# A decoder step in split fp32: where the upper MLP inverts its token factors, and in what order the lower MLP's first group loads and multiplies

## The chip, the cores and the metric

The kernel runs on one NeuronCore of a Trainium2 chip. The engines are TensorE (PE, with its weight loads apart as PEld), VectorE (DVE), ScalarE (ACT), GpSimd (POOL) and SyncE (SP), which issues most of the DMA transfers. The metric is the device time of one execution in microseconds; lower is better.

## The reference

One inference step of a decoder trunk with one layer, for 1024 prompt tokens and 8 sample tokens that share the weights: a hybrid of differential attention and retention, cross-attention into a memory, then the MLP that the change is about, and a last RMSNorm.

```python
def rmsnorm(x, g):
    y = xf * lax.rsqrt(jnp.mean(xf * xf, axis=-1, keepdims=True) + EPS)
    return (y * g.astype(jnp.float32)).astype(x.dtype)

def sq_relu_mlp(h, w_up, w_down):
    return jnp.square(jax.nn.relu(h @ w_up)) @ w_down
...
        xp = xp + sq_relu_mlp(rmsnorm(xp, norm_mlp[l]), w_up[l], w_down[l])
...
    y_prompt = rmsnorm(xp, norm_final)
```

D_MODEL is 1024, the hidden width 4096. All values are fp32.

## The kernel before, in words

**Number format.** Each fp32 operand is split in two parts, high and low (a cast on ScalarE, a subtraction on VectorE), and a product takes three matmuls: high by high, high by low, low by high. Names: `UH`/`UL` and `T_h`/`T_l` are right operands (activations, columns are tokens), `wu` and `wd` are split left operands (128 x 1024, high half and low half) of the upper and the lower MLP.

**Seven products.** Both MLP products use a variant of Strassen's scheme: the matrices are cut in 2 x 2 blocks, and seven products (numbers 1 to 7) take the place of eight. The tokens are 1032 columns, cut in two halves and each in two chunks c = 0, 1 of QC = 258.

**Upper MLP.** `up_block(b, W, chunks)` does block b of 16. For each product q in the order 1, 6, 2, 7, 5, 4, 3 and each chunk it runs 12 matmuls into a PSUM bank of kind `X` (products 1, 2), `Z` (6, 7, 4) or `Y` (5, 3), two banks of each. VectorE forms `u2` after product 6 and `u3` after 7, each of which must be read out before the next product may accumulate into that bank. `hidden(quad, src, c)` takes the relu, multiplies it by the token factor in `ssum` (one over the RMS of the token, since the norm is applied behind the product), and ScalarE squares it into `hq`. After product 3, `hidden` stores three quarters of `hq` to HBM (`HQ`, from ScalarE's queue), GpSimd forms four differences `ht` and stores them (`HT`). `norm_factor(x)` computes the token factors of a quarter of the columns: a matmul with ones, a square root on ScalarE, a reciprocal on VectorE. It is called for quarters 0 and 1 before block 0, and for 2 and 3 between chunk 0 and chunk 1 of block 0; blocks 1 to 15 run both chunks.

**Lower MLP.** Four groups g of the hidden width. In each, stages of products (1, 2), (6), (7, 4), (5, 3); within a stage pairs of tiles p (0, 1, then 2, 3), and chunks c. A step (q, p, c) is a chain of 12 matmuls, `lower`, called `dn` in the trace; products 1 and 2 of one (p, c) use one bank one after the other. In group 0 ScalarE copies product 1 to the accumulator `c0`, then product 2 goes on in the same bank; all other results VectorE adds to the accumulators `c0`, `c11`, `c21`, `c22`, `c12`, of which the last four are first loaded with the residual (`residual_rows`). Operands:

- `raw_d{g}_{p}_{x}`: the raw left operands, two loads of 512 KB for each p (x = 0, 1). `left_lower(g, p, q)` splits them to `wd` (ring of eight tiles); for product 6 it forms differences in place, on VectorE and GpSimd.
- `raw_h{g}_{q}_{kk}`: the raw right operand of product q in two loads (kk = 0, 2) from `HQ` or `HT`, through a ring of three raw tiles of which `raw_d0_1_1` holds one in group 0. `right_lower(g, q)` issues them on SP and splits them into one of four slots of `UH`/`UL`.

**What sets the order.** A scheduler places the instructions on the five queues by the dependencies between tiles, with the order of TensorE's matmuls in the MLP pinned to that of the program (`pinned`). `tc.issue_after(x)` keeps what follows behind instruction x in that order. Tiles with one tag share memory, so a tile's first write waits for the last use of the tile that had the place before. The tiles `xq2_0`, `xq3_0` hold `hq` and `xq2_1`, `xq3_1` hold `ht` of chunks 0 and 1 through the upper MLP. PSUM has eight banks; `acc` tiles of the lower MLP take them in turns, the first tile where the allocator puts it. By the addresses as built, the first eight are banks 0, 7, 6, 5, 4, 1, 2, 3, and the upper MLP has `X` in 2 and 3, `Z` in 4 and 5, `Y` in 6 and 7.

In group 0, of the left operands' loads those of p = 0 are issued on SP and those of p = 1, 2, 3 on GpSimd's queue, p = 2 and 3 in tiles `xq2_0`, `rd2`, `xq3_0`, `rd3`.

Of the kernel before, what the change touches and what calls it, by code (L numbers as in the profile page):

```python
# [2 lines left out]

# [45 lines left out]
def decoder_step(ctx: ExitStack, tc: tile.TileContext, i: dict, o: dict):  # L49
    nc = tc.nc  # L50

    def pool(name, bufs=1, space=None, side=None):
        if space is None:
            return tc.tile_pool(name=name, bufs=bufs, reuse_waits="tile", side=side)
        if space is PSUM:
            return tc.tile_pool(name=name, bufs=bufs, space=space, reuse_waits="tile")
        return tc.tile_pool(name=name, bufs=bufs, space=space)
# [1580 lines left out]
    def norm_factor(x):  # L1638
        cs = QCOLS[x]
        fp = PD.tile([P, 512], F32, tag=("mk", "dt")[x % 2], name=f"rm_{x}", bufs=1)[:, :QC]  # L1640
        mm(fp, onesq, ssum[:, cs], True, True)
        rf = ssum[:, cs]
        nc.scalar.activation(rf, fp, AF.Sqrt, scale=1.0 / D, bias=epsc)
        nc.vector.reciprocal(rf, rf)

    def first_half(c):

# [135 lines left out]

    def up_block(b, W, chunks):

        HQ_ = {}
        Z, X, Y, p1, u2, u3 = {}, {}, {}, {}, {}, {}

        def bank(kind, c):
            return SP.tile([P, 512], F32, tag=kind, name=f"{kind}_{b}_{c}", bufs=2)[:, :QC]  # L1790

        def small(kind, c, bufs=2):
            return HP.tile([P, QC], F32, tag=kind, name=f"{kind}_{b}_{c}", bufs=bufs)

        def hidden(quad, src, c):
            if c not in HQ_:
                if (b, c) == (0, 0):
                    HQ_[c] = N.tile([P, 4, QC], F32, tag="hq0", name="hq_0_0")
                else:
                    HQ_[c] = N.tile([P, 4, QC], F32, tag=f"xq{2 + c}_0", name=f"hq_{b}_{c}")  # L1800
            h = HQ_[c]
            r = small("r", f"{quad}_{c}", 4) if quad == 11 else src
            nc.vector.scalar_tensor_tensor(r, src, 0.0, ssum[:, QCOLS[2 * c + HALF_OF[quad]]], ALU.max, ALU.mult)  # L1803
            nc.scalar.activation(h[:, PLACE[quad], :], r, AF.Square)  # L1804
            if quad == 12:
                nc.scalar.dma_start(HQ[b, c].rearrange("p (x j) -> p x j", x=3), h[:, 0:3, :])
# [4 lines left out]
                nc.gpsimd.tensor_sub(t[:, 1, :], h22, t[:, 0, :])  # L1811
                nc.gpsimd.tensor_sub(t[:, 2, :], h22, h12)
                nc.gpsimd.tensor_sub(t[:, 3, :], h21, t[:, 1, :])
                nc.gpsimd.dma_start(HT[b, c].rearrange("p (x j) -> p x j", x=4), t)

        for q in (1, 6, 2, 7, 5, 4, 3):
            for c in chunks:
                if q in (1, 6, 5):
                    kind, d = {1: ("X", X), 6: ("Z", Z), 5: ("Y", Y)}[q]
                    d[c] = bank(kind, c)  # L1820
                ps = (X if q in (1, 2) else Z if q in (6, 7, 4) else Y)[c]
                product(W, q, c, ps, q in (1, 6, 5))
                if q == 1:
                    p1[c] = small("p1", c)
                    nc.scalar.copy(p1[c], ps)  # L1825
                elif q == 6:
                    u2[c] = small("u2", c)
                    nc.vector.tensor_add(u2[c], ps, p1[c])  # L1828
                elif q == 2:
                    hidden(11, ps, c)  # L1830
                elif q == 7:
                    u3[c] = small("u3", c)
                    nc.vector.tensor_add(u3[c], ps, p1[c])
                else:
                    quad, x = {5: (22, u3), 4: (21, p1), 3: (12, u2)}[q]
                    r = small("r", f"{quad}_{c}", 4)
                    nc.vector.tensor_add(r, ps, x[c])
                    hidden(quad, r, c)
# [29 lines left out]
    STAGES = [(1, 2), (6,), (7, 4), (5, 3)]  # L1868
    SOURCE = {1: (HQ, 0), 2: (HQ, 1), 3: (HQ, 2), 5: (HT, 0), 6: (HT, 1), 7: (HT, 2), 4: (HT, 3)}
    taken = [0, 0]  # L1870
    with pool("acc", side="right") as AC, pool("w") as A, pool("w_ps", space=PSUM) as PS:
# [6 lines left out]
        def residual_rows(quad):  # L1878
            kh, hs = {11: (0, lo_h), 21: (4, lo_h), 22: (4, hi_h), 12: (0, hi_h)}[quad]
            nc.sync.dma_start(C[quad], X3[kh : kh + 4, :, hs].rearrange("k p c -> p k c"))  # L1880


        FINISH_AT, tails = {2: (0, 0), 5: (1, 0), 9: (0, 1), 15: (1, 1)}, {}
# [61 lines left out]
        def finish(c, half):  # L1945
            tail = tails[c] if half else None
            cs = QCOLS[2 * c + half]
            fp = PS.tile([P, 512], F32, tag="acc", name=f"fin_{c}_{half}", bufs=8)[:, :QC]
            mm(fp, onesq, ssf[:, cs], True, tail is None)
            if tail is not None:  # L1950
                mm(fp, onesq, tail, False, True)
            rf = A.tile([P, QC], F32, tag="rf", name=f"rf_{c}_{half}", bufs=2)
            nc.scalar.activation(rf, fp, AF.Sqrt, scale=1.0 / D, bias=epsc)
            for ft in range(8):
                y = C[((11, 21), (12, 22))[half][ft // 4]][:, ft % 4, c * QC : c * QC + QC]
                nc.scalar.activation(y, y, AF.Copy, scale=g_fin[:, ft : ft + 1])
            nc.vector.reciprocal(rf, rf)
            for kh in range(2):
                y = C[((11, 21), (12, 22))[half][kh]][:, :, c * QC : c * QC + QC]
                nc.vector.tensor_mul(y, y, rf.unsqueeze(1).to_broadcast([P, 4, QC]))  # L1960
                nc.sync.dma_start(o["yT"][4 * kh * P : (4 * kh + 4) * P, cs].rearrange("(f p) c -> p f c", p=P), y)

        pin[0] = True
        for g in range(4):
            raws = {}
            for p in range(4):
                u = U_DN + 8 * g + 2 * p
                raws[p] = [
                    N.tile([P, 1024], F32, tag=("t2", "hq0", "xq2_0", "xq3_0")[p], name=f"raw_d{g}_{p}_0"),

                    G.tile([P, T], F32, tag="raw", name="raw_d0_1_1", bufs=3) if (g, p) == (0, 1)
                    else N.tile([P, 1024], F32, tag=("t3", "xq2_1")[p], name=f"raw_d{g}_{p}_1") if p < 2
                    else A.tile([P, 1024], F32, tag=f"rd{p}", name=f"raw_d{g}_{p}_1"),
                ]
            for p, x in ((0, 0), (0, 1), (1, 0), (1, 1), (2, 0), (2, 1), (3, 0), (3, 1)):

                (nc.gpsimd if g == 0 and p else nc.sync).dma_start(raws[p][x][:, :1024], i["wall"][U_DN + 8 * g + 2 * p + x])
            for stage in STAGES:
                if (g, stage[0]) == (0, 1):
                    residual_rows(11)  # L1980
                S = {q: right_lower(g, q) for q in stage}
                if (g, stage[0]) == (0, 7):

                    with tc.issue_after(seen["SP"]):
                        for quad in (22, 21, 12):
                            residual_rows(quad)
                end = g == 3 and stage == (5, 3)
                batches = [(0, 1), (2, 3)] if len(stage) == 2 else [(0, 1, 2, 3)]
                if end:
                    batches = [(0, 1, 2, 3)]  # L1990
                bank = {}
                steps = [(q, p, c) for batch in batches for q in stage for p in batch for c in range(2)]
                if end:
                    steps = [(q, p, c) for c in range(2) for q in stage for p in range(4)]
                W = {}
                for n, (q, p, c) in enumerate(steps):
                    if (q, p) not in W:
                        W[q, p] = left_lower(g, p, q)
                    if q == stage[0]:
                        bank[p, c] = PS.tile([P, 512], F32, tag="acc", name=f"dn_{g}_{q}_{p}_{c}", bufs=8)[:, :QC]  # L2000
                    ps = bank[p, c]
                    lower(W[q, p], S[q], c, ps, q == stage[0])
                    cq = slice(c * QC, c * QC + QC)
                    y = C[INTO[q]][:, p, cq]
                    if g == 0 and q == 1:
                        nc.scalar.copy(y, ps)
# [208 lines left out]
```

## Time and profile before

| | us |
|---|---|
| three runs | 1546.4, 1548.47, 1551.26 (median 1548.47) |
| profiled execution | 1553.3 |
| its span | 1551.5 |
| granted TensorE clock, mean | 0.988 |
| last product of the upper MLP ends, first of the lower starts | 1203.83 |

The table's first row is the measure. The profile is of another execution, 4.8 us longer than the median, and its clock readings (start, duration) count from the start of its span. In the rows, a line number such as L1928 is that of the kernel before, `out<-in` are the tiles by name without numbers, `x3` is the number of instructions in the row, and the last bracket tells how long the engine was idle before and which instruction's end released it.

### The profile page before, as it was taken

Reading aid. Unit: us, or ns where it says so; the run is one execution under the profiler, and the core shown is the slowest. Engines: PE = TensorE matmul, PEld = TensorE weight load, DVE = VectorE, ACT = ScalarE, POOL = GpSimd, SP = SyncE. Lnnn points to the kernel's source line nnn. Section 1 sums busy time; section 2 is a strip of 40 time slices with the busy share of each in tenths; the row PEclk is TensorE's granted clock in tenths of the full one; section 3 lists DMA queues with packets and bytes.
Section 4 is the critical chain, followed back from the end, with each engine's and each line's share of the span. In section 5 each row is a group of like instructions: output and inputs, shape, how many; then the busy total and the mean of one; then the engine's idle time right before and its main releaser. Section 6 shows DMA issues by size and latency. Waiting matters only on the chain.

```text
span 1551.5 us, 26774 instructions
## 1 busy us (share of the span) xinstructions
PE 1494.2 (96%) x10483; PEld 1394.0 (90%) x10483; DVE 1072.6 (69%) x2096; ACT 651.0 (42%) x1267; POOL 440.8 (28%) x461
## 2 busy tenths in 40 slices
PE   9899999999999899999999899999999899999997
PEld 7678869999759899988899899999999799999996
DVE  4324513988865735566696988888788688787887
ACT  6323323665642332046634643333334444334454
POOL 0343302122533421124222234443335402020360
PEclk9999999999999999999999999999999999999999
DMA  8645334212766156451583334434335873636313
GB/s 291 171 116 156 78 104 115 82 51 69 235 215 240 48 202 180 138 183 64 182 269 129 101 138 151 151 138 150 137 138 172 293 232 86 197 82 198 96 42 110
DMA packets 121874, 230.02 MB, mean 148 GB/s; under 512 B 14209, under 2 KB 74480, under 8 KB 121620
## 3 DMA queue, kind: packets, MB, share of 16 engines
q1 hardware_dynamic: 91508, 170.30, 35.3%
q0 software_dynamic: 21024, 41.10, 8.6%
q10 hardware_dynamic: 9216, 16.91, 2.9%
q8 instruction: 82, 1.34, 0.4%
q14 instruction: 44, 0.36, 0.1%
HBM read 168.93 MB, written 57.52 MB: 146 GB/s over the span
## 4 chain that ended last, share of the span: by engine, by line
PE 63%; DVE 17%; DMA 11%; ACT 4%; issue 3%; POOL 1%; SPq 0%; DVEq 0%; ACTq 0%; POOLq 0%
PE dn L1928 17%; PE Z L1778 5%; PE mq L67 5%; PE pr_o L67 4%; PE qkp L67 4%; PE Y L1778 4%; PE vrp L67 3%; PE vap L67 3%; DVE wu L1617 3%; PE grp L67 3%; DMA raw_up<-in_wall 3%; PE X L1778 2%; PE pr_m L67 2%; PE sp L67 2%; PE av L67 2%
## 5 line engine op out<-in xcount | busy, mean ns | idle before, releaser
L1928 PE MATMUL dn<-UH,wd 128*128 128x258 f32 x1792 | 326.1, 284 | 7.7 <-ACT wd L1906 4.3
L1928 PEld LDWEIGHTS dn<-UH,wd 128*128 128x128 f32 x1792 | 278.2, 190 | 9.2 <-ACT wd L1906 4.7
L1928 PE MATMUL dn<-UL,wd 128*128 128x258 f32 x896 | 253.3, 283 | 0.0
L1928 PEld LDWEIGHTS dn<-UL,wd 128*128 128x128 f32 x896 | 169.7, 189 | 0.1
L1804 ACT ACTIVATE hq<-r 128x258 f32<-128x258 f32 x128 | 53.5, 419 | 162.8 <-DVE r L1803 162.8
L2008 DVE TENSOR_TENSOR c<-c,dn 128x258 f32<-128x258 f32 x216 | 88.4, 418 | 35.5 <-PE dn L1928 33.4
L1778 PE MATMUL Z<-T_h,wu 128*128 128x258 f32 x512 | 100.0, 287 | 7.0 <-DVE u L1828 5.3
L1906 ACT CAST wd<-raw_d 128x512 fp32r<-128x512 f32 x96 | 58.9, 618 | 102.6 <-PE dn L1928 84.5
L1617 DVE TENSOR_TENSOR wu<-raw_up,wu 128x512 fp32r<-128x512 f32 x96 | 92.0, 959 | 9.2 <-ACT wu L1616 9.2
L1778 PE MATMUL X<-UH,wu 128*128 128x258 f32 x512 | 97.7, 282 | 0.4 <-ACT p L1825 0.4
L110 DVE TENSOR_TENSOR wl_u<-raw_u,wh_u 128x1024 fp32r<-128x1024 f32 x46 | 59.8, 1308 | 50.9 <-ACT wh_u L109 49.0
L1778 PEld LDWEIGHTS Z<-T_h,wu 128*128 128x128 f32 x512 | 81.4, 189 | 10.4 <-DVE u L1828 8.3
L1907 DVE TENSOR_TENSOR wd<-raw_d,wd 128x512 fp32r<-128x512 f32 x96 | 75.5, 790 | 14.3 <-ACT wd L1906 14.2
L1778 PEld LDWEIGHTS X<-UH,wu 128*128 128x128 f32 x512 | 81.3, 188 | 0.7 <-ACT p L1825 0.7
L1900 DVE TENSOR_TENSOR UL<-raw_h,UH 128x1032 fp32r<-128x1032 f32 x56 | 77.3, 1381 | 6.4 <-ACT UH L1899 6.4
L109 ACT CAST wh_u<-raw_u 128x1024 fp32r<-128x1024 f32 x50 | 52.3, 1050 | 69.9 <-PE mq L67 43.2
L1899 ACT CAST UH<-raw_h 128x1032 fp32r<-128x1032 f32 x56 | 58.8, 1055 | 52.0 <-PE dn L1928 30.9
L1810 POOL TENSOR_TENSOR ht<-hq 128x258 f32<-128x258 f32 x32 | 22.3, 698 | 202.1 <-ACT hq L1804 188.1
L1920 POOL TENSOR_TENSOR raw_d<-raw_d,raw_d 128x512 f32<-128x512 f32 x16 | 23.3, 1456 | 179.5 <-DVE raw_d L1916 164.0
L1778 PE MATMUL Z<-T_l,wu 128*128 128x258 f32 x256 | 72.3, 282 | 0.0
L1778 PE MATMUL X<-UL,wu 128*128 128x258 f32 x256 | 72.3, 282 | 0.0
L1616 ACT CAST wu<-raw_up 128x512 fp32r<-128x512 f32 x96 | 57.1, 610 | 30.4 <-DVE raw_up L1623 23.7
(482 smaller groups left out, 4634.6 us busy)
## 6 DMA issues: line engine op xcount, KB each, us to landing
raw_u<-in_wall SPq DMA_DIRECT2D x59, 512.0 KB
HT<-ht POOLq DMA_DIRECT2D x32, 516.0 KB
raw_h<-HT SPq DMA_DIRECT2D x32, 516.0 KB
raw_up<-in_wall SPq DMA_DIRECT2D x32, 512.0 KB
raw_d<-in_wall SPq DMA_DIRECT2D x26, 512.0 KB
HQ<-hq ACTq DMA_DIRECT2D x32, 387.0 KB
raw_h<-HQ SPq DMA_DIRECT2D x24, 516.0 KB
cmk<-in_cmk SPq DMA_DIRECT2D x16, 512.0 KB
```

Source lines behind the costliest of these rows:

```text
L67: pinned(nc.tensor.matmul(out, l, r, start=start, stop=stop))
L110: (lo_engine or nc.vector).tensor_sub(wl[:, :n], raw[:, :n], wh[:, :n].bitcast(F32))
L1616: nc.scalar.copy(w[:, :512], src)
L1617: nc.vector.tensor_sub(w[:, 512:], src, w[:, :512].bitcast(F32))
L1778: pinned(nc.tensor.matmul(ps, l, r[:, k, :], start=first and k == 0 and x == 0, stop=k == 3 and x == 2, skip_group_check=True))
L1804: nc.scalar.activation(h[:, PLACE[quad], :], r, AF.Square)
L1899: nc.scalar.copy(h, rv)
L1900: nc.vector.tensor_sub(l, rv, h.bitcast(F32))
L1906: nc.scalar.copy(w[:, :512], src)
L1907: nc.vector.tensor_sub(w[:, 512:], src, w[:, :512].bitcast(F32))
L1928: pinned(nc.tensor.matmul(ps, l, r[:, k, cq], start=first and k == 0 and x == 0, stop=k == 3 and x == 2, skip_group_check=True))
L2008: nc.vector.tensor_add(y, y, ps)
```

## The change

1. *Upper MLP.* The reciprocal leaves `norm_factor` for a new function `invert(x)`. For quarters 2c and 2c + 1 it is called in block 0, ahead of `hidden` of product 2 and behind `u3` of product 7.
2. *Upper MLP, last block.* The four differences `ht` of (b, c) = (15, 1) are formed on VectorE.
3. *PSUM.* The lower MLP's banks get eight tags, `acc0` to `acc7`, placed in order and used in turns. As built, the first eight are banks 0 to 7.
4. *Left operands of group 0.* All raw loads are issued on SP: p = 0, 1 first, p = 2, 3 behind the loads for product 6 and `c11` (now loaded in two halves). p = 2 gets tiles `rd2`, `rd3` of a pool of its own, p = 3 gets `xq2_0` and `xq3_0`. 
5. *Order of group 0.* (1, 2) on p = 0, 1; (6) on p = 0, 1; then for p = 2 and for p = 3 (1, 2) and (6). What follows is as before. `issue_after` puts the splits of p = 2, 3 and the operands of products 7 and 4 behind ScalarE's copies, and the loads of `c22`, `c21` and `c12` one by one behind the right operands.

```diff
         rf = ssum[:, cs]
         nc.scalar.activation(rf, fp, AF.Sqrt, scale=1.0 / D, bias=epsc)
-        nc.vector.reciprocal(rf, rf)
+
+    def invert(x):
+        nc.vector.reciprocal(ssum[:, QCOLS[x]], ssum[:, QCOLS[x]])
...
-                nc.gpsimd.tensor_sub(t[:, 0, :], h12, h11)
...
+                eng = nc.vector if (b, c) == (15, 1) else nc.gpsimd
+                eng.tensor_sub(t[:, 0, :], h12, h11)
...
                 elif q == 2:
+                    if b == 0:
+
+                        invert(2 * c)
                     hidden(11, ps, c)
                 elif q == 7:
                     u3[c] = small("u3", c)
                     nc.vector.tensor_add(u3[c], ps, p1[c])
+                    if b == 0:
+                        invert(2 * c + 1)
...
+        turns = [0]
+        for x in BANK_ORDER:
+            PS.tile([P, 512], F32, tag=f"acc{x}", name=f"acc{x}_order", bufs=1)
+
+        def acc_bank(name):
+            turns[0] += 1
+            return PS.tile([P, 512], F32, tag=f"acc{(turns[0] - 1) % 8}", name=name, bufs=1)[:, :QC]
...
+                tags = (("t2", "t3"), ("hq0", "xq2_1"), ("rd2", "rd3"), ("xq2_0", "xq3_0"))[p]
...
-                (nc.gpsimd if g == 0 and p else nc.sync).dma_start(raws[p][x][:, :1024], i["wall"][U_DN + 8 * g + 2 * p + x])
...
+            load_left((0, 1) if g == 0 else range(4))
+            S, W, bank, copied = {}, {}, {}, {}
+
+            parts = [((1, 2), (1, 2), (0, 1)), ((), (1, 2), (2, 3)), ((6,), (6,), (0, 1)), ((), (6,), (2, 3))]
+            if g == 0:
+
+                parts = [((1, 2), (1, 2), (0, 1)), ((6,), (6,), (0, 1))] + [((), qs, (p,)) for p in (2, 3) for qs in ((1, 2), (6,))]
+            parts += [((7, 4), (7, 4), (0, 1)), ((), (7, 4), (2, 3)), ((5, 3), (5, 3), (0, 1)), ((), (5, 3), (2, 3))]
...
+                if g == 0 and 7 in new:
+
+                    for q, quad in ((7, 22), (4, 21)):
+                        with tc.issue_after(seen["SP"]), tc.issue_after(copied[2]):
+                            S[q] = right_lower(g, q)
+                        with tc.issue_after(seen["SP"]):
+                            residual_rows(quad)
...
+                if g == 0 and 1 in new:
+                    residual_rows(11, (slice(0, 2),))
+                if g == 0 and 6 in new:
+                    residual_rows(11, (slice(2, 4),))
+                    load_left((2, 3))
...
+                        with tc.issue_after(copied[p - 1]) if g == 0 and p > 1 else nullcontext():
+                            W[q, p] = left_lower(g, p, q)
...
                     if g == 0 and q == 1:
                         nc.scalar.copy(y, ps)
+                        copied[p] = nc.cur_bb.bb.instructions[-1]
```

VectorE in block 0, where chunk 1 begins; `ssum3` are the token factors, `T41_l` the low part of a right operand of product 4. Before:

```order
L1644 RECIPROCAL ssum3_7431<-ssum3_7431 128x258
L1636 TENSOR_TENSOR T41_l_8659<-xq_2_1_7428,T41_h_8658 128x516
L1644 RECIPROCAL ssum3_7431<-ssum3_7431 128x258
L1828 TENSOR_TENSOR u2_0_1_8857<-Z_0_1_8844,p1_0_1_8842 128x258
L1803 SCALAR_TENSOR_TENSOR r_0_11_1_8872<-X_0_1_8829,ssum3_7431 128x258
```

The same place after:

```order
L1646 RECIPROCAL ssum3_7431<-ssum3_7431 128x258
L1636 TENSOR_TENSOR T41_l_8659<-xq_2_1_7428,T41_h_8658 128x516
L1831 TENSOR_TENSOR u2_0_1_8855<-Z_0_1_8842,p1_0_1_8840 128x258
L1805 SCALAR_TENSOR_TENSOR r_0_11_1_8871<-X_0_1_8827,ssum3_7431 128x258
L1646 RECIPROCAL ssum3_7431<-ssum3_7431 128x258
L1839 TENSOR_TENSOR u3_0_1_8886<-Z_0_1_8842,p1_0_1_8840 128x258
```

The second of the two reciprocals has moved behind `r_0_11_1`; those of chunk 0 are where they were.

SP's queue from the right operands of product 6 on, before:

```order
L1893 DMA raw_h0_6_0_13172<-HT_74 128x4x258
L1893 DMA raw_h0_6_2_13176<-HT_74 128x4x258
L1880 DMA c11_12893<-X3_72 128x4x516
L1893 DMA raw_h0_7_0_13324<-HT_74 128x4x258
L1893 DMA raw_h0_7_2_13328<-HT_74 128x4x258
L1893 DMA raw_h0_4_0_13332<-HT_74 128x4x258
L1893 DMA raw_h0_4_2_13336<-HT_74 128x4x258
L1880 DMA c22_12895<-X3_72 128x4x516
```

The same queue after:

```order
L1911 DMA raw_h0_6_0_13059<-HT_74 128x4x258
L1911 DMA raw_h0_6_2_13063<-HT_74 128x4x258
L1898 DMA c11_12904<-X3_72 128x2x516 x2
L1996 DMA raw_d0_2_0_12914<-in_wall 128x1024
L1996 DMA raw_d0_2_1_12915<-in_wall 128x1024
L1996 DMA raw_d0_3_0_12916<-in_wall 128x1024
L1996 DMA raw_d0_3_1_12917<-in_wall 128x1024
L1911 DMA raw_h0_7_0_13336<-HT_74 128x4x258
L1911 DMA raw_h0_7_2_13340<-HT_74 128x4x258
L1898 DMA c22_12906<-X3_72 128x4x516
L1996 DMA raw_d1_1_1_13854<-in_wall 128x1024
L1911 DMA raw_h0_4_0_13345<-HT_74 128x4x258
```

The left operands of p = 2 and 3 stand between `c11` and product 7, and a load of group 1, `raw_d1_1_1`, ahead of product 4's.

ScalarE around the two copies of p = 3, before:

```order
L2006 COPY c0_12897<-dn_0_1_3_0_13086 128x258
L1906 CAST wd0_2_6_13255<-s2_0_2_13252 128x512
L1899 CAST UH_66<-raw_h0_4_0_13332 128x2x516
L2006 COPY c0_12897<-dn_0_1_3_1_13100 128x258
L1899 CAST UH_66<-raw_h0_4_2_13336 128x2x516
```

The same place after:

```order
L1924 CAST wd0_2_7_13474<-raw_d0_2_0_12914 128x512
L2045 COPY c0_12908<-dn_0_1_3_0_13243 128x258
L1917 CAST UH_66<-raw_h0_4_0_13345 128x2x516
L2045 COPY c0_12908<-dn_0_1_3_1_13257 128x258
L1924 CAST wd0_3_7_13505<-raw_d0_3_0_12916 128x512
L1917 CAST UH_66<-raw_h0_4_2_13349 128x2x516
```

The cast of product 4's first half stands between the two copies in both; the cast for product 6 of p = 2 has gone ahead.

More of the change, by code (lines that the diff above doesn't have):

```diff
@@ L1867, in decoder_step @@
     SLOTS = [(HALVES[x], HALVES[x + 4]) for x in range(4)]
-    STAGES = [(1, 2), (6,), (7, 4), (5, 3)]
+    BANK_ORDER = range(8)
     SOURCE = {1: (HQ, 0), 2: (HQ, 1), 3: (HQ, 2), 5: (HT, 0), 6: (HT, 1), 7: (HT, 2), 4: (HT, 3)}
     taken = [0, 0]
-    with pool("acc", side="right") as AC, pool("w") as A, pool("w_ps", space=PSUM) as PS:
+    with pool("acc", side="right") as AC, pool("rd", side="right") as RD, pool("w") as A, pool("w_ps", space=PSUM) as PS:
+        turns = [0]
[4 more added lines that the diff above has]
+            return PS.tile([P, 512], F32, tag=f"acc{(turns[0] - 1) % 8}", name=name, bufs=1)[:, :QC]
         C = {}
@@ L1947, in finish @@
             cs = QCOLS[2 * c + half]
-            fp = PS.tile([P, 512], F32, tag="acc", name=f"fin_{c}_{half}", bufs=8)[:, :QC]
+            fp = acc_bank(f"fin_{c}_{half}")
             mm(fp, onesq, ssf[:, cs], True, tail is None)
@@ L1975, in decoder_step @@
[L1975 to L1982, printed above, removed]
-                    with tc.issue_after(seen["SP"]):
[L1985 to L1988, printed above, removed]
-                if end:
[L1990 to L1995, printed above, removed]
+                    G.tile([P, T], F32, tag="raw", name="raw_d0_1_1", bufs=3) if (g, p, x) == (0, 1, 1)
+                    else (RD if p == 2 else N).tile([P, 1024], F32, tag=tags[x], name=f"raw_d{g}_{p}_{x}")
@@ new lines, in decoder_step, with load_left @@
+                    for x in range(2)
+                ]
+            def load_left(pairs):
+                for p in pairs:
+                    for x in range(2):
+                        nc.sync.dma_start(raws[p][x][:, :1024], i["wall"][U_DN + 8 * g + 2 * p + x])
+                seen["SP"] = nc.cur_bb.bb.instructions[-1]
+            load_left((0, 1) if g == 0 else range(4))
+            S, W, bank, copied = {}, {}, {}, {}
+            parts = [((1, 2), (1, 2), (0, 1)), ((), (1, 2), (2, 3)), ((6,), (6,), (0, 1)), ((), (6,), (2, 3))]
```

36 lines of the change are left out of this document (22 added, 14 removed).

## The prediction

> **What bounds the kernel now.** I read the page's busy times and its chain of waits first, then the waits of TensorE by the line that it waited for, then the chain that ended last in order of time.
>
> ```profile
> PE 1494.2 (96%) x10483; PEld 1394.0 (90%) x10483; DVE 1072.6 (69%) x2096; ACT 651.0 (42%) x1267; POOL 440.8 (28%) x461
> PE 63%; DVE 17%; DMA 11%; ACT 4%; issue 3%; POOL 1%; SPq 0%; DVEq 0%; ACTq 0%; POOLq 0%
> ...
> PE Z L1778 <- DVE u L1828: 5.3, 6, 1.9
> PE dn L1928 <- ACT wd L1906: 4.3, 2, 2.9
> PE dn L1928 <- DVE r L1837: 2.1, 1, 2.1
> PE dn L1928 <- DVE wd L1907: 0.6, 1, 0.6
> ...
> 1235.30 242.43 PE dn L1928 x2022
> ```
>
> TensorE is busy 96% of the span, so only its idle time can be won. The third to sixth row are waits of TensorE: us in all, times, longest. The three of `dn` belong to the first group of the lower MLP; from 1235.30 on TensorE runs unbroken for 242 us, at 242.43 / 2022 = 0.12 us from one matmul to the next (1.44 us for a chain of 12). What can be won lies in front of 1235.30. Windows of 10 us show where (us, then busy time and count of TensorE, weight loads, VectorE, ScalarE, GpSimd; then granted clock, DMA share, GB/s):
>
> ```profile
> 760.00:770.00 10.00, 10.00 (x73) 10.00 (x73) 5.94 (x13) 5.00 (x13) 0.00 (x0) 0.84 0.54 175
> 880.00:890.00 10.00, 8.08 (x64) 7.77 (x63) 10.00 (x16) 3.60 (x9) 3.88 (x6) 1.00 0.48 152
> 1200.00:1210.00 10.00, 7.91 (x65) 7.70 (x65) 6.31 (x13) 5.66 (x11) 2.32 (x4) 1.00 0.99 307
> 1220.00:1230.00 10.00, 7.26 (x42) 6.62 (x43) 6.99 (x11) 4.34 (x9) 3.02 (x2) 0.83 1.04 398
> 1240.00:1250.00 10.00, 10.00 (x86) 10.00 (x85) 9.63 (x18) 4.20 (x6) 0.00 (x0) 1.00 0.78 233
> ```
>
> The full pace is the last row, 86 matmuls. The two stretches that the change touches, 880 to 890 and 1200 to 1230, fall to 64, 65 and 42, and in one of them the clock is 0.83.
>
> **Term 1, the reciprocals.** In the order as built only one instruction that matters moves: the fourth reciprocal leaves its place ahead of `u2` of chunk 1 and stands behind `r_0_11_1`. The two of chunk 0 and the third stay where they were.
>
> ```profile
> 885.24 0.28 PE L1778 MATMUL X<-UH,wu 128*128 128x258 f32 x1
> 887.43 0.38 PE L1778 MATMUL Z<-T_h,wu 128*128 128x258 f32 x1 [1.92 <-DVE u L1828]
> ...
> 885.33 1.76 DVE L1644 RECIPROCAL ssum<-ssum 128x258 f32<-128x258 f32 x1
> 887.00 0.38 DVE L1828 TENSOR_TENSOR u<-Z,p 128x258 f32<-128x258 f32 x1
> ```
>
> TensorE loses 887.43 - 885.24 - 0.12 = 2.07 us, because `u` stands behind the reciprocal on VectorE. Without it `u` starts at 885.33 in place of 887.00: 1.67 us are won, 0.40 stay. The reciprocal then stands behind `r_0_11_1` and ahead of `u3`. With the end of product 2 as zero, it ends at 0.4 + 1.76 = 2.2 and `u3` at 2.6; TensorE wants `u3` after products 7 and 5, at 2 x 1.44 = 2.9. So 0.3 us cover it; the splits of block 1's weights behind it have the same total ahead of them as before. I book 1.67; bounds: 0 (the 1.76 us come back as that wait) and 2.07.
>
> **Term 2, the PSUM banks.** The third chain of the lower MLP was given the bank that the last addition of the upper MLP still had to read.
>
> ```profile
> 1203.83 0.28 PE L1928 MATMUL dn<-UH,wd 128*128 128x258 f32 x1
> 1205.15 0.28 PE L1928 MATMUL dn<-UH,wd 128*128 128x258 f32 x1
> 1207.52 0.39 PE L1928 MATMUL dn<-UH,wd 128*128 128x258 f32 x1 [2.09 <-DVE r L1837]
> ...
> 1207.04 0.42 DVE L1837 TENSOR_TENSOR r<-Y,u 128x258 f32<-128x258 f32 x1
> ```
>
> The loss is 1207.52 - 1205.15 - 0.12 = 2.25 us. After the change the first group takes banks 0 to 7 in order, and the two banks of `Y` (6 and 7) are the seventh and eighth that it opens, with its chains 11 and 12, that is from 1203.83 + 10 x 1.44 = 1218.2 on, 11 us behind the read at 1207.04. VectorE gets more in front of that read (three operations for the sixth product's weights that stood later before, about 0.7 us each); 11 us cover it. Without the cover the cost would be the 2.25 again. I book 2.25; lower bound 0.
>
> **Term 3, the left operands of tile pairs 2 and 3.** Before, their four raw loads are issued by GpSimd behind its eight subtractions, and pair 2 is wanted as ninth chain.
>
> ```profile
> 1214.54 0.56 POOL L1977 DMA_DIRECT2D raw_d<-in_wall  x1
> 1215.64 1.60 POOL L1977 DMA_DIRECT2D raw_d<-in_wall  x3
> ...
> 1215.64 8.54 DMA raw_d<-in_wall
> ...
> 1220.09 0.62 ACT L1906 CAST wd<-raw_d 128x512 fp32r<-128x512 f32 x1 [6.24 <-DMA raw_d<-in_wall]
> ...
> 1217.57 0.28 PE L1928 MATMUL dn<-UH,wd 128*128 128x258 f32 x1
> 1220.76 0.58 PE L1928 MATMUL dn<-UH,wd 128*128 128x258 f32 x1 [2.91 <-ACT wd L1906]
> 1225.23 0.28 PE L1928 MATMUL dn<-UH,wd 128*128 128x258 f32 x1
> 1226.91 0.39 PE L1928 MATMUL dn<-UH,wd 128*128 128x258 f32 x1 [1.40 <-ACT wd L1906]
> 1227.14 0.28 PE L1928 MATMUL dn<-UL,wd 128*128 128x258 f32 x1
> 1228.00 0.51 PE L1928 MATMUL dn<-UH,wd 128*128 128x258 f32 x2 [0.58 <-DVE wd L1907]
> ```
>
> TensorE loses 3.07 + 1.56 + 0.74 = 5.37 us (start to start, less 0.12). Afterwards pair 2 is the thirteenth chain, wanted at 1203.83 + 12 x 1.44 = 1221.1, and pair 3 the nineteenth, 1229.8. Pair 2's tiles now only wait for the last upper product that reads a T operand, about 1201; with the 8.54 us of the row above they land at 1209.5, and cast and split (0.62 + 0.69) end 10 us early. Pair 3's tiles wait for the last subtraction of `ht_15_0`, about 1212 on GpSimd before, and no later now that it has four subtractions in place of eight: 1212 + 8.54 + 1.3 = 1221.9, 8 us early. The four subtractions that VectorE takes over (some 0.4 each) delay nothing that is due before 1215. I book 5.37; lower bound 0.
>
> **Term 4, the clock.** In 1220 to 1230 the granted clock is 0.83, so 0.17 x 10 = 1.7 us of that window's pace are missing beside the idle time. It comes right behind the 2.91 us wait. Another such window, 760 to 770 at 0.84, comes behind a wait of 2.05:
>
> ```profile
> 759.49 0.99 PE L70 MATMUL mtr<-ident,me 128*128 128x128 f32 x4 [2.05 <-DVE me L1471]
> ```
>
> With the waits the window should go: 1.7. Bounds 0 and 1.7. The other side: waits of 1.92 (887.43) and 2.09 (1207.52) were followed by clocks of 1.00, so a wait alone does not decide it. The Trainium skill, "TensorE: Matmul & The Clock Gate", Part 1, puts the low state behind an idle window of about 3.4 us; by that rule the wait of 2.91 would not have caused it, and 1.7 us might stay, which would give 1539.2. The trace agrees only in the duration being a few us; the low clock behind 2.05 speaks against the threshold.
>
> **Term 5, a wait that changes its cause.** On ScalarE the cast of product 4's right operand, `raw_h0_4_0`, stands between the two copies of pair 3's first chains, before and after, and chain 22 waits for the second copy. Before, the operand had long landed (SP had issued its load by 1216), and the pair of matmuls that opens the chain took 0.75 us in place of 0.4: the copy ended at 1235.24, and some 0.3 us were lost.
>
> ```profile
> 1233.93 1.05 ACT L1899 CAST UH<-raw_h 128x1032 fp32r<-128x1032 f32 x1
> 1234.88 0.36 ACT L2006 COPY c<-dn 128x258 f32<-128x258 f32 x1
> 1234.93 0.75 PE L1928 MATMUL dn<-UH,wd 128*128 128x258 f32 x2
> ...
> 1236.07 1.23 DVE L1900 TENSOR_TENSOR UL<-raw_h,UH 128x1032 fp32r<-128x1032 f32 x1
> 1237.32 3.59 SPq L1893 DMA_DIRECT2D raw_h<-HT  x2
> 1241.09 1.06 ACT L1899 CAST UH<-raw_h 128x1032 fp32r<-128x1032 f32 x1 [2.72 <-DMA raw_h<-HT]
> ```
>
> After, the load comes late: it needs a ring buffer that VectorE's split of `raw_h0_7_0` frees, and this split stands behind the addition for chain 16. The last three rows are the same hand-over one product later, before the change: the load is issued as the split ends (1237.30), and its cast starts 3.77 us after the issue. Chain 16 ends at 1203.83 + 16 x 1.44 = 1226.9; addition, one subtraction and split (0.4 + 0.7 + 1.23) take it to 1229.2, the load to 1233.0, cast and copy (1.06 + 0.36) to 1234.4. Chain 22 is due at 1203.83 + 21 x 1.44 = 1234.1: a wait of 0.3, as long as before. If the load takes the 8.54 us of term 3's row, the wait is 1237.7 + 1.4 - 1234.1 = 5.0, that is 4.7 more. I take the nearest row, the same tensor on the same queue: a change of 0, bounds 0.3 won and 4.7 lost. Product 7's right operands are due at 1238.4 (chain 25) and product 4's second half, issued when `raw_h0_7_2` is split near 1231, at 1244.2 (chain 29): 13 us.
>
> What else is edited costs nothing that I can find: the loads, casts and order of the groups after the first are the same, and they lie beside TensorE's unbroken stretch.
>
> **The sum.** 1.67 + 2.25 + 5.37 + 1.7 + 0 = 11.0 us. The profiled execution took 1553.3 (span 1551.5), so it would be 1542.3; it lies 4.8 above the median of the runs, 1548.47, which gives 1537.5 as the forecast.
>
> **The rivals.**
> - The low clock stays, or the load of term 5 is slow. For it: the two rows of 1.00 behind waits of 2 us; or the busy queue, 398 GB/s in 1220 to 1230. Term 4 at 0 gives 1548.47 - 9.3 = 1539.2; term 5 at 4.7 lost gives 1542.2.
> - VectorE gives it back. It gets the subtractions and the splits earlier, and shares its time with GpSimd: of one and the same operation the trace has 3.36 and 1.23 us.
>
> ```profile
> 1193.54 3.36 DVE L1900 TENSOR_TENSOR UL<-raw_h,UH 128x1032 fp32r<-128x1032 f32 x1
> 1204.30 1.23 DVE L1900 TENSOR_TENSOR UL<-raw_h,UH 128x1032 fp32r<-128x1032 f32 x1 [0.18 <-ACT UH L1899]
> ```
>
>   One such stretch on the path costs 2.1; or the reciprocal gives term 1 back, 1.7. Either gives about 1539.4. Against it: each has 8 us of cover, but for the reciprocal.
> - The change does not do what it says for the left operands: SP works in order, and pairs 2 and 3 stand behind two loads into `c11` and a wait for TensorE. If they land as late as before in relation to their use, terms 3 and 4 are gone and only 1.67 + 2.25 are left: 1544.6. Against it: they would have to be 8 us later than worked out.
> - Slower: on SP a load for the second group, `raw_d1_1_1`, stands ahead of `raw_h0_4_0`, and its tile is free only when the store of `ht_15_0` to HBM has landed. Were that store held up among the other transfers, chain 22 would wait for it one for one. The wait eats all 11.0 us when `raw_h0_4_0` lands at 1233.0 + 11.0 = 1244.0, and the kernel is slower by 0.3% (4.6 us, about what a measurement here can tell) when it lands at 1248.6, giving 1553.1. The store is issued near 1212 and would have to take over 30 us, where loads take 3.77 and 8.54.
>
> **How the numbers follow.** My forecast's case 0.45; low clock stays 0.14; slow load in term 5 0.10; VectorE gives back 0.15; left operands late 0.12; slower 0.04. The bound of 0.3% lies at 1543.8: all cases but the last two are under it, and about 0.01 of the slow load is over: faster 0.83, same 0.13, slower 0.04. The range reaches from 1533.5 (term 1 at its upper bound, 0.4, and 3.6 of the 4.9 us by which the three runs differ, since the new median is as unsure as the old) to 1545.0, which takes in all the cases but the slower one. The forecast's own range is 1534 to 1540.
>
> **What would show it.** The wait at 887 falls to about 0.3; the wait for `r` near 1207 and those for `wd` near 1220 to 1228 are gone; the clock is 1.00 all through the first group; TensorE has one small wait near chain 22, for ScalarE. The prediction is wrong if `dn` waits for `wd` or for ScalarE's copy by over 3 us there, or if a wait of the reciprocal's length turns up in blocks 0 and 1.

## The result and the profile after

| | before | after |
|---|---|---|
| median of the runs, us | 1548.23 (1544.84 to 1551.26) | 1539.64 (1534.92 to 1543.33) |
| ratio, 95% interval | | 0.9945 [0.992, 0.9969] |
| span of the profiled execution, us | 1551.5 | 1537.8 |

The change made the kernel faster by 8.6 us; the forecast was 1537.5, 11.0 us under before. The page after has TensorE one per cent busier and less VectorE, DMA and ScalarE in the chain of waits:

```profile
PE 1493.9 (97%) x10483; PEld 1395.9 (91%) x10483; DVE 1075.8 (70%) x2100; ACT 652.6 (42%) x1267; POOL 431.6 (28%) x451
PE 75%; DVE 12%; DMA 6%; ACT 3%; issue 3%; POOL 1%; SPq 0%; DVEq 0%; ACTq 0%; POOLq 0%
```

TensorE's waits from the lower MLP's first chain to its last (us in all, times, longest). The wait for `r` and all waits for `wd` are gone; the first group has one wait left, for ScalarE's copy:

```profile
PE fin L67 <- DVE ssumf L1961: 1.7, 1, 1.7
PE dn L1946 <- ACT c L2045: 1.4, 1, 1.4
PE dn L1946 <- DVE c L2048: 0.6, 1, 0.6
```

The windows after (busy times and counts, then clock, DMA share, GB/s): 1200 to 1220 is at the full 86 matmuls, the clock is 1.00 from 1200 on, and 880 to 890 has 81 in place of 64. But 910 to 920, which no term of the prediction speaks of, has 64, and in 920 to 930 the clock is 0.83, with 71 matmuls.

```profile
880.00:890.00 10.00, 9.71 (x81) 9.50 (x80) 9.99 (x18) 3.79 (x9) 3.35 (x5) 1.00 0.71 231
910.00:920.00 10.00, 7.55 (x64) 7.35 (x63) 8.36 (x11) 3.03 (x7) 7.03 (x9) 1.00 0.43 152
920.00:930.00 10.00, 10.00 (x71) 10.00 (x72) 7.49 (x16) 3.42 (x8) 0.73 (x2) 0.83 0.13 54
1200.00:1210.00 10.00, 10.00 (x86) 10.00 (x85) 9.41 (x18) 3.81 (x10) 5.03 (x7) 1.00 0.70 230
1210.00:1220.00 10.00, 10.00 (x86) 10.00 (x86) 4.78 (x9) 2.26 (x5) 1.71 (x2) 1.00 1.05 394
1220.00:1230.00 10.00, 8.75 (x74) 8.54 (x72) 10.00 (x15) 6.76 (x12) 3.45 (x2) 1.00 0.29 81
```

The last of these stretches of the upper MLP before:

```profile
920.00:930.00 10.00, 9.64 (x81) 9.44 (x80) 8.63 (x16) 3.65 (x9) 3.44 (x5) 1.00 0.27 107
```

Kernels that are the same up to the upper MLP reach it at anything from 861.5 to 871.4 us of their profiles, so profiles are compared by stretches between three matmuls: the one that a wait for `xs` releases where the upper MLP begins, the first of the lower MLP, and its last. After, with the two waits for `u` and the first matmul of product 5 of block 2 between:

```profile
866.52 0.35 PE L1780 MATMUL Z<-UH,wu 128*128 128x258 f32 x1 [1.23 <-DVE xs L1749]
882.74 0.39 PE L1780 MATMUL Z<-T_h,wu 128*128 128x258 f32 x1 [0.29 <-DVE u L1831]
919.98 0.39 PE L1780 MATMUL Z<-T_h,wu 128*128 128x258 f32 x1 [2.44 <-DVE u L1831]
924.44 0.30 PE L1780 MATMUL Y<-T_h,wu 128*128 128x258 f32 x1
1198.45 0.28 PE L1946 MATMUL dn<-UH,wd 128*128 128x258 f32 x1
1230.17 0.38 PE L1946 MATMUL dn<-UH,wd 128*128 128x258 f32 x1 [1.42 <-ACT c L2045]
1526.54 0.28 PE L1946 MATMUL dn<-UH,wd 128*128 128x258 f32 x1
```

And the rows of before that answer to the first, third, fourth and last (the others stand in the prediction):

```profile
869.58 0.35 PE L1778 MATMUL Z<-UH,wu 128*128 128x258 f32 x1 [1.29 <-DVE xs L1747]
922.75 0.39 PE L1778 MATMUL Z<-T_h,wu 128*128 128x258 f32 x1 [0.36 <-DVE u L1828]
925.75 0.28 PE L1778 MATMUL Y<-T_h,wu 128*128 128x258 f32 x1
1540.27 0.28 PE L1928 MATMUL dn<-UH,wd 128*128 128x258 f32 x1
```

The lower stretch fell from 1540.27 - 1203.83 = 336.44 to 1526.54 - 1198.45 = 328.09 us. In the upper one the wait in block 0 shrank from 1.92 to 0.29, but the next row down grew from 0.36 to 2.44: from the wait for `xs` to that row it was 53.17 us before and is 53.46 after. That row is product 7 of block 2, where VectorE forms `u` only behind splits of block 3's weights; the expectations below call it block 3's wait. Behind it the clock is low after the change, so product 5, which is 24 matmuls further, starts 56.17 us behind the wait for `xs` before and 57.92 us behind it after: by there the change has lost 1.75 us.

All kernels that were run, by the same three matmuls. The ratio is to the kernel before, timed beside it on the same chip:

| kernel | `xs` to first lower chain, us | first to last lower chain, us | ratio, 95% interval |
|---|---|---|---|
| before | 334.25 | 336.44 | 1 |
| after | 331.93 | 328.09 | 0.9945 [0.992, 0.9969] |
| after, again | 333.21 | 327.91 | 0.9932 [0.991, 0.9955] |
| recip_only | 335.95 | 336.59 | 1.0005 [0.9987, 1.0024] |
| no_recip | 332.60 | 327.95 | 0.9921 [0.9891, 0.9952] |
| no_fourth | 329.08 | 328.33 | 0.9924 [0.9901, 0.9947] |
| banks_only | 333.59 | 338.94 | 0.9979 [0.9961, 0.9997] |
| banks_again | 332.86 | 339.05 | one run |
| old_chains | 334.00 | 330.04 | 0.9947 [0.9921, 0.9972] |
| pool_queue | 333.52 | 328.18 | 0.9943 [0.9915, 0.9971] |
| late_loads | 333.89 | 329.36 | 0.996 [0.9936, 0.9984] |
| copy_first | 332.62 | 327.52 | 0.9938 [0.9918, 0.9957] |
| early_raw | 329.97 | 327.66 | 0.9925 [0.9897, 0.9954] |
| early_raw_again | 328.85 | 327.88 | 0.9917 [0.9887, 0.9948] |

The lower stretch repeats within 0.3 us where nothing in it differs. The upper one does not: seven profiles with the moved reciprocal and the usual loads (after twice, recip_only, copy_first, pool_queue, old_chains, late_loads) lie from 331.93 to 335.95. Up to product 5 of block 2 the profiles are far closer: in those seven it starts 57.4 to 58.3 us behind the wait for `xs`, in the four with the reciprocal in its old place (before, no_recip, banks_only, banks_again) 55.7 to 56.4. Each of the seven has a wait of 2.05 to 3.02 us in front of it and 1.7 us of pace missing by a low clock around the end of that wait; in the other profiles of the table the clock is 1.00 there.

### The profile page after: what moved, and what is told of

It is laid out like the page before. It is cut to its first block, busy times and chain, and to the rows that moved or that the text cites. A ratio compares the mean times of both kernels' runs of the same rounds, so it can differ in the third digit from the quotient of the medians.

```text
span 1537.8 us, 26785 instructions
## 1 busy us (share of the span) xinstructions
PE 1493.9 (97%) x10483; PEld 1395.9 (91%) x10483; DVE 1075.8 (70%) x2100; ACT 652.6 (42%) x1267; POOL 431.6 (28%) x451
## 4 chain that ended last, share of the span: by engine, by line
PE 75%; DVE 12%; DMA 6%; ACT 3%; issue 3%; POOL 1%; SPq 0%; DVEq 0%; ACTq 0%; POOLq 0%
PE dn L1946 18%; PE Z L1780 7%; PE mq L67 5%; PE Y L1780 5%; PE X L1780 4%; PE pr_m L67 4%; PE pr_o L67 4%; PE qkp L67 4%; PE vrp L67 3%; PE vap L67 3%; PE grp L67 3%; PE sp L67 2%; PE av L67 2%; PE mpv L67 1%; DVE dacc L1218 1%
```

## The experiments

### Is the reciprocal's 1.67 us kept?

recip_only is before with this edit alone, no_recip is after with it undone:

```diff
-        nc.vector.reciprocal(rf, rf)
+    def invert(x):
+        nc.vector.reciprocal(ssum[:, QCOLS[x]], ssum[:, QCOLS[x]])
...
+                    if b == 0:
+                        invert(2 * c)
...
+                    if b == 0:
+                        invert(2 * c + 1)
```

recip_only. 

> The kernel before with the reciprocal's move alone. Theory of the prediction: the wait for u in block 0 falls from 1.92 to some 0.3 us and the 1.67 us stay won: from the wait for xs to the first matmul after block 3's wait for u the time falls from 53.2 to 51.5. Rival: there the pace is VectorE's and the raw_up loads', which it releases; the wait in block 0 falls too, but the wait for u where block 3 begins grows from 0.36 to about 2.2, the stretch stays at 53.2 +- 0.5, and the whole time at 1548 +- 3. In both the lower MLP keeps its waits (2.1 for r, 2.9 + 1.4 for wd).

no_recip. 

> The kernel after with the reciprocals put back into norm_factor. Theory of the prediction: 1.67 us are lost, from the wait for xs to the first lower chain 331.9 -> 333.6. Rival, VectorE and its loads set the pace there: the wait in block 0 is 1.9 again, but block 3's falls from 2.44 to about 0.5, and the stretch stays at 331.9 +- 0.7.

In recip_only the wait in block 0 fell to 0.29 and the next rose to 3.02:

```profile
880.21 0.39 PE L1780 MATMUL Z<-T_h,wu 128*128 128x258 f32 x1 [0.29 <-DVE u L1830]
918.03 0.58 PE L1780 MATMUL Z<-T_h,wu 128*128 128x258 f32 x1 [3.02 <-DVE u L1830]
```

From the wait for `xs` (863.99) to the second row it is 54.04 us, against 53.17 in before. The time is unchanged, 1.0005; by its interval, -2.0 to +3.7 us, a gain of 1.67 would still be possible, so the rows decide. no_recip shows the mirror image: 1.91 in block 0, 0.23 at the second place, and 332.60 us to the first lower chain, within what after's two profiles show. So the 1.67 us were won at one place and lost 37 us later, and the low clock behind the second place took as much again. Over the whole upper stretch no difference is left that the spread would show: the means are 333.6 for the seven with the move and 333.3 for the four without. Where the rest of the upper MLP makes up for it was not followed.

What sets the second place? VectorE waits there for `raw_up`, the raw weights of block 3. First before, then after:

```profile
913.68 0.69 DVE L1621 TENSOR_TENSOR s<-raw_up,raw_up 128x512 f32<-128x512 f32 x1 [0.86 <-DMA raw_up<-in_wall]
```

```profile
910.92 0.69 DVE L1621 TENSOR_TENSOR s<-raw_up,raw_up 128x512 f32<-128x512 f32 x1 [2.79 <-DMA raw_up<-in_wall]
```

Counted from the wait for `xs` this operation starts at 44.10 us before and at 44.40 after: TensorE came earlier, the weights did not. The chain that ended last, in order of time, gives the reason (after):

```profile
905.59 0.60 DVE wu L1617
...
906.22 4.61 DMA raw_up<-in_wall
...
910.92 0.69 DVE s L1621
```

The load is issued when VectorE's last split of the block before frees the ring buffer; it lands 4.6 us later, and the next splits start. TensorE does not stand in these rows, so a stall taken from TensorE alone need not bring the next load forward. In the same chain of before the loads of blocks 2 and 3 are

```profile
896.05 4.55 DMA raw_up<-in_wall
...
909.73 3.86 DMA raw_up<-in_wall
```

that is, they leave 26.5 and 40.2 us behind the wait for `xs`; after, they leave at 28.3 and 39.7. With the moved reciprocal block 2's load leaves 1.8 us later. Block 3's leaves 0.5 us earlier and takes 4.61 us in place of 3.86; why it takes longer was not tested. Two runs test the loop: one takes work from VectorE, one takes the ring out of the loop.

no_fourth (after, without the fourth reciprocal):

```diff
-                    if b == 0:
+                    if b == 0 and c == 0:
                         invert(2 * c + 1)
```

> The kernel after, with the fourth reciprocal left out (the last quarter of the tokens is multiplied by the root in place of its inverse). Theory of the prediction: behind r_0_11_1 the reciprocal was covered, so leaving it out wins 0 to 0.3 us; the stretch from the wait for xs to block 3's first Z after its wait for u stays at 53.5. Rival, VectorE as the bound there: 1.0 to 1.8 us less, 51.7 to 52.5, and the wait for u at block 3 falls from 2.44 to 0.7 to 1.4.

The wait at the second place is gone from the list; what is left of TensorE's waits for `u` from 868.66 to 923.66 is

```profile
PE Z L1780 <- DVE u L1831: 1.2, 2, 0.9
PE Z L1780 <- DVE u L1839: 0.4, 1, 0.4
```

The matmul of the second place starts 51.83 us behind the wait for `xs` (863.66), where the rival had 51.7 to 52.5:

```profile
915.49 0.39 PE L1780 MATMUL Z<-T_h,wu 128*128 128x258 f32 x1
```

That is 1.63 us earlier than in after. With the stall the low clock is gone too, which no expectation had: product 5 starts at 54.83, 3.1 us earlier than in after, and the upper stretch is 329.08, 2.85 less.

early_raw (the change to `copied` is that of copy_first, below):

```diff
-        ra, rb = (G.tile([P, T], F32, tag="raw", name=f"raw_up{b}_{x}", bufs=3) for x in range(2))
+        ra, rb = (N.tile([P, 1024], F32, tag=f"t{2 + x}", name=f"raw_up2_{x}") if b == 2
+                  else G.tile([P, T], F32, tag="raw", name=f"raw_up{b}_{x}", bufs=3) for x in range(2))
```

> The kernel after, with product 4's operand behind the last copy and the raw weights of upper block 2 in two tiles that are free at that time, in place of ring buffers, so that the loads of blocks 2 and 3 don't wait for VectorE's last split of the block before. If the loop split - ring buffer - load is what set the time of block 3, VectorE's 2.8 us of waiting for raw_up go, block 3's wait falls from 2.4 to under 0.7, and the stretch from the wait for xs to the first lower chain falls from 331.9 to about 330; whole time 3 us under that of after. If VectorE's own work is the bound, the wait stays above 1.7.

> The kernel with early raw weights and the copy first, again, beside the kernel after on the same chip: first lower chain near 330 after the wait for xs, first to last 327.6; the whole time 2.5 us under that of after.

The second load of block 2 and that of block 3 now leave SP at (first profile)

```profile
873.65 0.33 SPq L1611 DMA_DIRECT2D raw_up<-in_wall  x1
...
889.86 0.33 SPq L1611 DMA_DIRECT2D raw_up<-in_wall  x1
```

that is 12.1 and 28.3 us behind the wait for `xs` (861.55). In after the same two leave 28.3 and 39.7 us behind it: the second in the chain above, the first at

```profile
894.81 0.33 SPq L1610 DMA_DIRECT2D raw_up<-in_wall  x1
```

VectorE no longer waits for `raw_up` in this stretch, the wait at the second place is gone in both profiles, the clock stays at 1.00, and product 5 starts at 53.76 in both, 2.4 us ahead of before. The upper stretch is 329.97 and 328.85. So the loop through the ring buffer is what took the reciprocal's gain back. The medians are 1538.7 and 1537.03, against 1541.04 for the second measurement of after, which ran beside the latter; the intervals of the two overlap, so the profiles show 2 to 4 us gained in the upper MLP and the timed runs do not contradict it. The two profiles have the shortest spans here, 1530.5 and 1529.5 us; the timed runs do not set this kernel apart, since no_recip and no_fourth have ratios as low.

### Do the terms of the lower MLP add up?

banks_only is before with the bank tags:

```diff
+        def acc_bank(name):
+            turns[0] += 1
+            return PS.tile([P, 512], F32, tag=f"acc{(turns[0] - 1) % 8}", name=name, bufs=1)[:, :QC]
...
-                        bank[p, c] = PS.tile([P, 512], F32, tag="acc", name=f"dn_{g}_{q}_{p}_{c}", bufs=8)[:, :QC]
+                        bank[p, c] = acc_bank(f"dn_{g}_{q}_{p}_{c}")
```

> The kernel before with the order of the PSUM banks alone. Theory of the prediction, terms that add up: the wait for r goes, 2.25 us won, first to last lower chain 336.4 -> 334.2. Rival: the left operand of pair 2 lands when it lands; TensorE only comes to it earlier, the wait of 2.9 for wd grows to 5.1, and the stretch stays at 336.4 +- 0.5 or grows if the longer idle time brings more of the low clock.

> The kernel with the banks alone, a second profile. If the 7.8 us wait for wd there was the rule, it is 5 to 8 us again and first to last lower chain 336 to 339; if one late load, it is near 5.1 and the stretch near 336.4, or under it.

The wait for `r` is gone, and the one for `wd` is 7.64 (7.81 in the second profile) in place of 2.91; the clock falls behind it (banks_only):

```profile
1221.29 0.58 PE L1936 MATMUL dn<-UH,wd 128*128 128x258 f32 x1 [7.64 <-ACT wd L1914]
```

```profile
1210.00:1220.00 10.00, 3.66 (x30) 3.36 (x28) 1.97 (x2) 0.74 (x3) 5.70 (x10) 0.81 0.98 309
1220.00:1230.00 10.00, 7.76 (x39) 7.12 (x40) 6.65 (x11) 4.02 (x9) 2.68 (x2) 0.68 1.03 407
```

That is 1.9 + 3.2 = 5.1 us of pace missing (some of it while TensorE waited), three times the 1.7 of before; the second profile has 0.74 and 0.75 in these windows, which is 5.1 again. So term 2 alone is worth nothing in the profile: TensorE reaches a load 2.25 us earlier that does not land earlier. It even lands later:

```profile
1213.02 0.56 POOL L1985 DMA_DIRECT2D raw_d<-in_wall  x1
```

```profile
1220.62 0.62 ACT L1914 CAST wd<-raw_d 128x512 fp32r<-128x512 f32 x1 [9.88 <-DMA raw_d<-in_wall]
```

From issue to cast that is 7.60 us, and 5.55 in before (1214.54 to 1220.09). Why it lands later was not tested. Both profiles have the lower stretch 2.5 us longer than before, while the ratio of the timed runs is 0.9979, with an interval that just leaves out 1. The profiled executions, 1553.84 and 1551.65 us, are slower than the median of 1547.89 and need not be typical; the contradiction stays open.

What carries term 3: the queue, the earlier loads, or the later place of the chains? Three variants of after:

```diff
-                        nc.sync.dma_start(raws[p][x][:, :1024], i["wall"][U_DN + 8 * g + 2 * p + x])
+                        (nc.gpsimd if g == 0 and p > 1 else nc.sync).dma_start(raws[p][x][:, :1024], i["wall"][U_DN + 8 * g + 2 * p + x])
...
```

pool_queue, the edit above; left out is that `seen["SP"]`, behind which later loads are kept, stays at the last load of p = 1, since the others are no longer on SP. 

> The kernel after with the raw left operands of pairs 2 and 3 issued by GpSimd again, tiles and order of the chains as after. If the queue had been the cause, pair 2 is late again: waits for wd of 2 to 5 us, first to last lower chain 330 to 333. If the tiles (no wait for the hq tiles, so that GpSimd issues pair 2 ahead of its subtractions) and the later place of the chains were it: no wait for wd, 328.1 +- 0.6.

```diff
-                eng = nc.vector if (b, c) == (15, 1) else nc.gpsimd
+                eng = nc.gpsimd
...
-                tags = (("t2", "t3"), ("hq0", "xq2_1"), ("rd2", "rd3"), ("xq2_0", "xq3_0"))[p]
+                tags = (("t2", "t3"), ("hq0", "xq2_1"), ("xq2_0", "rd2"), ("xq3_0", "rd3"))[p]
...
-                    else (RD if p == 2 else N).tile([P, 1024], F32, tag=tags[x], name=f"raw_d{g}_{p}_{x}")
+                    else (RD if p > 1 and x else N).tile([P, 1024], F32, tag=tags[x], name=f"raw_d{g}_{p}_{x}")
```

late_loads, both edits. 

> The kernel after with the left operands of pairs 2 and 3 as before: tiles xq2_0, rd2, xq3_0, rd3, issued by GpSimd, and all eight subtractions on GpSimd in front of the first of them. Banks and order of the chains as after. If the order of the chains alone covers them: issue at 11.3 us after the first chain, as before, landing 5.5 us later, cast and split 1.3: 18.1 against 17.3 when chain 13 is due, a wait for wd of 0.8, none for pair 3, first to last lower chain 329 +- 0.6. If the earlier loads carry term 3: waits of 2 to 5 us, 330 to 333.

```diff
-                parts = [((1, 2), (1, 2), (0, 1)), ((6,), (6,), (0, 1))] + [((), qs, (p,)) for p in (2, 3) for qs in ((1, 2), (6,))]
+                pass
...
+                    load_left((2, 3))
                 if g == 0 and 6 in new:
...
-                    load_left((2, 3))
```

old_chains, this last edit alone (`c11` is loaded whole ahead of the left operands). 

> The kernel after with group 0's chains in the order of before ((1, 2) on pairs 0, 1, 2, 3, then (6)), the loads as after. Pair 2 is due 11.5 us after the first chain and lands before; pair 3 is due 14.4 less 1.3 us after it (near 1211.6 in the clock of the profile after), its load issued at 1206.2. If it takes 8.5 us, TensorE waits 3: first to last lower chain 330 to 331. If it takes 4, the loads alone had been enough: 327 to 328.5, and the wait at chain 22 is gone as well.

TensorE's waits in the first group, one fence for each in this order:

```profile
PE dn L1946 <- ACT c L2049: 1.5, 1, 1.5
```

```profile
PE dn L1946 <- ACT c L2049: 2.0, 1, 2.0
```

```profile
PE dn L1946 <- DVE c L2046: 1.7, 1, 1.7
PE dn L1946 <- ACT wd L1924: 1.0, 1, 1.0
PE dn L1946 <- DVE wd L1925: 0.2, 1, 0.2
```

The queue is worth nothing (328.18 against 328.09 and 327.91). With the loads as late as before, the order of the chains leaves no wait for `wd`: 329.36. With the order of before, the earlier loads leave 1.2 us for `wd` and bring a wait of 1.7 for an addition into `c`, later in the group: 330.04. With the banks, the order alone brings 7.1 of the 8.4 us and the loads alone 6.4; both cover the same stall, which is why each looked necessary.

### The wait that is left

copy_first:

```diff
-                        with tc.issue_after(seen["SP"]), tc.issue_after(copied[2]):
+                        with tc.issue_after(seen["SP"]), tc.issue_after(copied[2 if q == 7 else 3]):
```

> The kernel after, with product 4's right operand behind ScalarE's last copy in place of the copy of pair 2. Theory: the wait of 1.42 us at chain 22 is the copy standing behind the cast, which waits for the load; it goes, and first to last lower chain falls from 328.1 to 326.6. Rival: the operand of product 4 then is late at chain 29, or the wait has another cause, and the stretch stays at 328.1 +- 0.4.

The wait at chain 22 is gone and the first 50 us of the lower MLP have no wait at all. The stretch fell to 327.52, 0.4 to 0.6 under after's two profiles and not 1.5: the gain is a third of what was expected. It was there at first: counted from the start of the first chain, chain 22 starts at 30.14 us in place of 31.72 and 31.56. It shrinks to 0.4 to 0.6 within the next 50 us. There TensorE falls short of its full pace, with 82, 82 and 84 matmuls in the three windows from 1251 to 1281 where after has 86 in each, and only one wait, of 0.18, is long enough to be listed; what holds it there was not tested. The cause of the wait is shown; its worth for the stretch is 0.4 to 0.6, and the timed runs (0.9938 against 0.9945 and 0.9932) can't tell.

## Why the prediction was right or wrong

- **Term 1, forecast 1.67, measured nothing.** The local step was right: the loss at that matmul fell from 2.07 to 882.74 - 882.17 - 0.12 = 0.45 us, so 1.62. The step that failed is the one behind it: "the splits of block 1's weights behind it have the same total ahead of them as before". In time that did not hold: the split that frees the ring buffer for block 2's second load ends 1.8 us later with the moved reciprocal (load at 28.3 us in place of 26.5), and block 3's weights came no earlier than before (44.40 against 44.10), so TensorE, which came earlier, met them with a stall of 2.44 us. The step also looked no further than block 1, and had no low clock behind the new stall: by product 5 of block 2 the change is 1.75 us behind in the profile after. Over the whole upper stretch neither a gain nor a loss is clear of the spread. The rival "VectorE gives it back" had the price for the term (1539.4), with a wait of the reciprocal's length; the signs named blocks 0 and 1, and it turned up in block 2.
- **Term 2, forecast 2.25, and term 3, forecast 5.37:** both stalls are gone, and the cover was as computed: pair 2's cast ran at 1204.64, 6.2 us behind the first chain, where chain 13 was due at 17.3. But the two are not independent terms. The first stall alone is worth nothing in the profiles, as banks_only shows; their sum came out because the load was covered in the same change.
- **Term 4, forecast 1.7: right for the lower MLP.** The clock is 1.00 in all windows from 1200 on, so the rival in which the low clock stays there is refuted. But the moved stall of term 1 brought one low stretch of the same size to the upper MLP (0.83 in 920 to 930), and the mean clock of the two profiles is the same, 0.988. That the clock follows the waits is supported by the longer wait in banks_only, which brought 0.81 and 0.68, and by no_fourth and early_raw, where the stall at the second place is gone and the low clock with it.
- **Term 5, forecast no change, measured 1.3 lost:** TensorE lost 1230.17 - 1228.47 - 0.12 = 1.58 us in place of 0.3. The mechanism was right and the load's time too, 1228.80 - 1224.99 = 3.81 against 3.77:

```profile
1224.99 3.60 SPq L1911 DMA_DIRECT2D raw_h<-HT  x2
```

```profile
1228.80 1.05 ACT L1917 CAST UH<-raw_h 128x1032 fp32r<-128x1032 f32 x1 [2.49 <-PE dn L1946]
1229.75 0.37 ACT L2045 COPY c<-dn 128x258 f32<-128x258 f32 x1
```

  The bracket names TensorE, which had long been done with that slot; the load is what came last. Mis-sized was the issue: 26.5 us behind the first chain in place of 25.4. The subtraction ahead of the split took 1.68 and not 0.7, at a time when GpSimd worked on the same pair's raw tiles; that makes up 1.0 of the 1.1 (what slowed it was not tested):

```profile
1222.14 1.68 DVE L1935 TENSOR_TENSOR s<-raw_d 128x512 f32<-128x512 f32 x1
1223.74 1.22 DVE L1918 TENSOR_TENSOR UL<-raw_h,UH 128x1032 fp32r<-128x1032 f32 x1
```

```profile
1221.98 1.29 POOL L1938 TENSOR_TENSOR raw_d<-raw_d,raw_d 128x512 f32<-128x512 f32 x1 [9.57 <-DVE raw_d L1934]
```

- **The sum.** With term 1 at 0 and term 5 at -1.3 it is 2.25 + 5.37 + 1.7 - 1.3 = 8.0; the lower stretch shows 8.35 and the medians 8.6. Two of five terms were off by 3.0 us in all; that the time still fell in the forecast's own range of 1534 to 1540, near its end, owes something to the width of that range. The profiles differ by 13.7 us in span, of which 3.1 lie ahead of the change (869.58 - 866.52) and 2.3 in the upper stretch, which varies by as much between executions of kernels that are equal there.
- **Slower, left operands late:** neither came. The store that the slower rival needed to be 30 us late did not show as a wait.

## What to carry to other kernels

When a stall of the bounding engine is to be taken away, find the loop that paces the stretch: follow the buffer that the stalled operand lives in back to what frees it. If that loop (here split, ring buffer, load, split) runs without the bounding engine, the stall moves on by a few blocks and the time stays, and a stall that has moved can bring a low clock where the old one did not; taking work or a buffer out of the loop is what gains. Waits in a row for one late load are one term, not several, and two remedies for one stall should be tried apart before both are kept.

## What the runs showed of the hardware that was not expected

Between the start of the upper MLP and 1240 us the granted clock was low only around and behind waits, and each time by the same amount or a multiple: 0.83 in a window of 10 us is 1.7 us of pace, and the low windows of banks_only and banks_again make three times that. The length of one wait does not decide it. In recip_only a wait of 1.75 us at 1203.29 was followed by a low clock (0.83 in 1200 to 1210, the row below), while before kept 1.00 behind waits of 1.92 at 887.43 and 2.09 at 1207.52. All waits of 2.3 us and more in these stretches were followed by one, after's 2.44 too (0.83 in 920 to 930).

```profile
1200.00:1210.00 10.00, 8.25 (x56) 8.05 (x56) 5.75 (x10) 5.20 (x12) 6.53 (x9) 0.83 0.84 264
```
